# A planner that books a shared port from the third mixer on

## The chip, the cores and the metric

One core of one Trainium2 chip runs the kernel. The metric is the device time of one execution in microseconds; the time before is the median of three runs, 1043.78 us (1042.79 to 1044.37).

## The reference, cut to what matters

The reference is two transformer blocks on 256 tokens of width 1024. The first block has two layers: a mixer (FoX attention and sparse latent attention in the first, block attention in the second) and a feed-forward net with a short convolution. The second block has one layer, and the change begins with its mixer:

```python
c_q, c_kv, k_r, x_m, z, i_pre, f_pre = _split_in(h @ w_in[i])
attn_out = _mla_attention(q_nope, q_rope, k_nope, k_rope, v)      # 8 heads, run in 4 pairs
xc = jax.nn.silu(_causal_conv(x_m, conv_w[i], conv_b[i]))
hm = _mlstm_chunkwise(mq, mk, mv, ig, fg)                         # 4 heads
x = x + jnp.concatenate([attn_out, ml_out], axis=-1) @ w_o[i]
x = x + _hier_moe(...)                                            # 32 experts, 2 per token
x = x + (p[i] @ w_ple[i]) * jax.nn.sigmoid(hp @ w_ple_gate[i])
```

All is computed in float32; large products split each weight and each activation into a high and a low part and add three products (high by high, high by low, low by high).

## The kernel before, in words

The kernel is one straight program for 256 tokens. Activations lie with features on the partitions, weights stream from HBM through slots in SBUF (`Weights`, lines 209 to 346). For each unit of 1024 columns ScalarE casts the high part (`high`, line 291) and VectorE subtracts to get the low part (`low`, line 300). `W.eighths` says how many eighths of a low part go to GpSimd instead; it is 0 in the third mixer's dense products and 4 in the first half of its output projection (line 1159).

In a mixer the dense products (`product`, line 987) run on TensorE, and between them stand steps of side work. Each chain of side work is a Python generator: `mla` for a pair of attention heads (lines 1815 and 1085), `lstm_inputs` for the convolution and its Silu (line 1706), `mlstm` for an mLSTM head (line 1850), `lstm_outputs` and `gate_tiles` for its normalization and gate, `scale_x` for scaling the residual X (line 1662). `tick` (line 432) is called after every six matmuls of a dense product. It goes through the list of chains in order of priority and takes the next step of the first chains whose last result is foreseen to be ready by the foreseen time of TensorE (line 447), at most one step per tick here (`MOST`). `pause` (line 453) does the same with nothing else to issue, and moves the time on by 0.1 us if no chain is ready. So the order of instructions in every engine's queue is fixed when the program is built, by foreseen times.

The foreseen times come from `Clock` (line 64). `cost` (line 123) gives the duration of an operation by engine and columns, `issue` (line 148) starts it when its engine is free and its operands are ready, and `LATE` (line 67) is added before another engine may use the result. For n columns VectorE is given 0.07 + 0.00104 n us (0.0007 n for a copy or a scaling in SBUF) and GpSimd 0.1 + 0.0022 n; a matmul of 256 columns has 0.109. Engines do not disturb each other in `issue`.

The order of weight casts is decided apart: `prepare` (line 320) issues casts when the weights are there and a small number of units is ahead, and `take` (line 342) forces the unit that is to be used.

After the third mixer come the output projection with the router's inputs (`out_proj`, `to_moe`), the routing, a stage of 32 experts in a written order, and a last gated product. The numbers of most experts to load are known only after the routing (`order_of_use`, line 2142); until then only the first six experts' weights can be fetched.

Of the kernel before, what the change touches and what calls it, by code (L numbers as in the profile page):

```python
# [18 lines left out]
PSUM = bass.MemoryType.PSUM  # L19
# [44 lines left out]
class Clock:  # L64
# [6 lines left out]
    def __init__(self):  # L71
        self.at = dict.fromkeys(("pe", "act", "dve", "pool", "sp", "dma"), 0.0)
        self.log, self.rings, self.gone = {}, {}, set()
        self.last = self.floor = 0.0
        self.table, self.off = "-", False
        self.duty = {}

    def now(self):
        return max(self.at["pe"], self.floor)
# [43 lines left out]
    def cost(self, eng, what, outs, ins, func):  # L123
        n = max(self.size(x) for x in outs + ins)
        if eng == "pe":
            n = self.size(outs[0])
            if ins[0].dtype in (F32R, BF):
                return (max(n, 64) * 0.417e-3 + 0.0023) * (4 if n < 256 and ins[0].dtype == F32R else 1)
            if what == "transpose":
                return 0.109  # L130
            if self.box(outs[0])[0] >= 32:

                return 0.03
            return max(0.096, n * 1.667e-3 + 0.0023)
        if eng == "act":
            t = self.TABLES.get(func)
            c = (0.027 if ins[0].space == PSUM else 0.045) + n * 0.887e-3 + 0.1 * (len(ins) - 1) + 0.09 * (len(outs) - 1)
            if t and self.table not in t:
                self.table = t[0]
                c += 1.28  # L140
            return c
        if eng == "dve":
            mild = what in ("tensor_scalar", "tensor_copy") and all(x.space != PSUM for x in outs + ins)
            more = 0.06 if what != "tensor_tensor" and not mild and any(self.size(x) == 1 for x in ins) and n > 1 else 0
            return 0.07 + n * (0.7e-3 if mild else 1.04e-3) + more
        return 0.1 + n * 2.2e-3

    def issue(self, eng, what, outs, ins, func=None):
        for x in outs + ins:
            if x.tensor.name in self.gone:  # L150
                raise RuntimeError(f"{x.tensor.name} has been given up")
        if self.off:
            return
        s = max([self.at[eng]] + [self.ready(x, False, eng) for x in ins] + [self.ready(x, True, eng) for x in outs])
        if eng == "sp":
            self.at["sp"] = s + 0.45
            n = math.prod(c for _, c in outs[0].ap) * 4
            end = max(s + 1.2, self.at["dma"]) + n / 2 ** 20 * 2.91
            self.at["dma"] = end
            late = end + 0.5  # L160
        else:
            c = self.cost(eng, what, outs, ins, func)
            if eng == "pe":
                w = int(s / self.WINDOW)
                self.duty[w] = self.duty.get(w, 0.0) + c
                if self.duty.get(w - 1, 0.0) < self.BUSY * self.WINDOW:
                    c *= 2
            end = s + c
            late = end + self.LATE[eng]
            self.at[eng] = end  # L170
            self.last = max(self.last, late)
        for x in ins:
            self.note(x, False, end, late, eng)
        for x in outs:
            self.note(x, True, end, late, eng)
# [178 lines left out]
def tile_two_blocks(ctx: ExitStack, tc: tile.TileContext, a: dict, out: bass.AP):  # L354
    clk = Clock()
# [5 lines left out]
    def st(shape, dt=F32, tag=None, name=None, bufs=1):  # L361
        return sb.tile(list(shape), dt, tag=tag or name, name=name or tag, bufs=bufs)
# [238 lines left out]
    for i, g in enumerate(ORDER0):  # L601
        n = ORDER0[:i].count(g)
# [960 lines left out]
    for i, g in enumerate(ORDER0):  # L1563
        n = ORDER0[:i].count(g)
# [77 lines left out]


    lay[0] = W.phase = 2
    r4 = st([128, 4], name="r4")

    def norm_twice():
# [945 lines left out]
```

## Time and profile before

| | us |
|---|---|
| median of three runs | 1043.78 |
| profiled execution | 1051.57 |
| its span | 1049.9 |
| TensorE busy | 987.1 (94%) |
| VectorE busy | 620.6 (59%) |
| ScalarE busy | 479.7 (46%) |
| GpSimd busy | 98.1 (9%) |
| mean granted clock of TensorE | 0.968 of full speed |

PE is TensorE, PEld its weight loads, DVE is VectorE, ACT is ScalarE, POOL is GpSimd, SP issues the DMAs. Times in the views are in microseconds from the start of the span. Nearly all instructions have the line 205, that of a helper which records them, so they are told apart by the names of the tiles: `out<-in`. In the third mixer aP and aPT are softmax tiles, aQ and aR queries, keys and their rotations, bX and bZ the tiles of the mLSTM, `extra`, `wh`, `wl`, `xhw`, `xlw` high and low parts of weights, and `more` a wide tile with tables and masks.

### The profile page before, as it was taken

The numbers are of one execution on the slowest core, as the hardware profiler recorded it, in microseconds if no ns is written. First come the engines' busy times: TensorE is split into PE (matmuls) and PEld (weight loads), VectorE is DVE, ScalarE is ACT, GpSimd is POOL, SyncE is SP. The second block draws the span as 40 slices with busy tenths as digits, with TensorE's granted clock in tenths as the row PEclk, the third lists the DMA queues.
The fourth block names the chain that finished last, engine by engine and source line by source line (L and its number), as shares of the span: only waits on it lengthen the run. The fifth ranks groups of instructions, "written<-read, shape, count | busy, mean of one in ns | idle before, by whom it ended". The sixth has DMA issues, their size and how long they took to land.

```text
span 1049.9 us, 19301 instructions
## 1 busy us (share of the span) xinstructions
PE 987.1 (94%) x7612; PEld 851.0 (81%) x7612; DVE 620.6 (59%) x1285; ACT 479.7 (46%) x868; POOL 98.1 (9%) x183
## 2 busy tenths in 40 slices
PE   7999999999999999999999999979889999788697
PEld 7988899999999998999999999857775454343276
DVE  5698576666678588676666687685463122111046
ACT  5555565444555465564544465664422111111063
POOL 7414120000001000000000000040310000000001
PEclk8999999999999999999999999988889999998898
DMA  7563299564610632597556103423579899999961
GB/s 217 168 201 118 85 327 344 172 224 152 226 42 3 199 123 79 192 368 243 191 171 206 63 1 105 137 81 138 208 263 397 334 413 409 413 410 412 410 214 41
DMA packets 135313, 223.10 MB, mean 213 GB/s; under 512 B 11161, under 2 KB 103473, under 8 KB 135217
## 3 DMA queue, kind: packets, MB, share of 16 engines
q1 hardware_dynamic: 134673, 221.80, 59.3%
q8 instruction: 62, 1.02, 0.4%
q14 instruction: 34, 0.28, 0.1%
q10 hardware_dynamic: 544, 0.00, 0.0%
HBM read 220.73 MB, written 1.05 MB: 211 GB/s over the span
## 4 chain that ended last, share of the span: by engine, by line
PE 75%; DMA 12%; DVE 9%; ACT 3%; issue 1%; SPq 0%; POOL 0%; DVEq 0%; ACTq 0%
PE bank L205 75%; DMA w<-in_w_gate_e_dram 6%; DMA w<-in_w_down_e_dram 3%; DMA w<-in_w_up_e_dram 2%; DVE a L205 1%; DMA w<-in_w_in_even_dram 1%; DVE wl L205 1%; DVE X L205 1%; DVE mx L205 1%; DVE xl L205 1%; DVE extra L205 1%; DVE aR L205 1%; DVE gates L205 1%; DVE m L205 0%; ACT wh L205 0%
## 5 line engine op out<-in xcount | busy, mean ns | idle before, releaser
L205 PE MATMUL bank<-xh,wh 128*128 128x256 f32 x808 | 231.4, 286 | 3.1 <-ACT wh L205 3.1
L205 PE MATMUL bank<-xl,wh 128*128 128x256 f32 x808 | 226.4, 280 | 0.3 <-DVE xl L205 0.3
L205 PE MATMUL bank<-xh,wl 128*128 128x256 f32 (+1 forms) x752 | 211.2, 281 | 1.0 <-DVE wl L205 1.0
L205 ACT ACTIVATE wh<-w 128x1024 fp32r<-128x1024 f32 x153 | 159.8, 1051 | 6.2 <-PE bank L205 5.3
L205 PEld LDWEIGHTS bank<-xh,wh 128*128 128x128 f32 x808 | 153.6, 190 | 5.4 <-ACT wh L205 3.3
L205 PEld LDWEIGHTS bank<-xl,wh 128*128 128x128 f32 x808 | 153.4, 190 | 1.4 <-issue 0.7
L205 PEld LDWEIGHTS bank<-xh,wl 128*128 128x128 f32 (+1 forms) x752 | 142.4, 189 | 1.4 <-DVE wl L205 1.4
L205 PE MATMUL bank<-xh,extra 128*128 128x256 f32 (+1 forms) x552 | 141.9, 283 | 0.0
L205 DVE TENSOR_TENSOR wl<-w,wh 128x1024 fp32r<-128x1024 f32 (+2 forms) x102 | 120.1, 1178 | 8.0 <-ACT wh L205 6.5
L205 PE MATMUL bank<-w,xg 128*32 128x512 f32 (+1 forms) x512 | 93.4, 645 | 18.6 <-DMA w<-in_w_up_e_dram 12.4
L205 PEld LDWEIGHTS bank<-xh,extra 128*128 128x128 f32 (+1 forms) x552 | 98.6, 187 | 1.0 <-issue 0.9
L205 ACT ACTIVATE c<-more,v,cw 128x256 f32<-128x256 f32 x44 | 26.5, 603 | 137.6 <-DVE more L205 137.6
L205 PEld LDWEIGHTS bank<-w,xg 128*32 128x32 f32 (+1 forms) x512 | 30.3, 127 | 72.7 <-issue 71.5
L205 DVE TENSOR_TENSOR more<-bank,more 128x512 f32<-128x512 f32 x44 | 30.4, 692 | 80.5 <-PE bank L205 80.5
L205 PE MATMUL bank<-al,wh 128*128 128x256 f32 x256 | 71.5, 279 | 0.0
L205 PE MATMUL bank<-ah,wh 128*128 128x256 f32 x256 | 71.4, 279 | 0.0
L205 POOL TENSOR_TENSOR sq<-sq 128x512 f32<-128x512 f32 (+1 forms) x14 | 16.0, 1144 | 582.3 <-ACT sq L205 397.3
L205 PE MATMUL bank<-xl,extra 128*128 128x256 f32 (+2 forms) x248 | 69.8, 281 | 0.0
L205 DVE SCALAR_TENSOR_TENSOR sg<-sg,ws,bank 128x256 f32<-128x256 f32 x11 | 5.3, 481 | 107.1 <-ACT sg L205 107.1
L205 PE MATMUL bank<-ah,extra 128*128 128x256 f32 x256 | 65.6, 280 | 0.0
L205 DVE TENSOR_TENSOR extra<-w,wh 128x1024 fp32r<-128x1024 f32 (+2 forms) x51 | 60.8, 1192 | 3.3 <-ACT wh L205 3.3
L205 ACT ACTIVATE extra<-w 128x1024 fp32r<-128x1024 f32 (+4 forms) x54 | 53.5, 996 | 1.0 <-PE bank L205 0.9
(483 smaller groups left out, 2165.9 us busy)
## 6 DMA issues: line engine op xcount, KB each, us to landing
w<-in_w_up_dram SPq DMA_DIRECT2D x44, 1024.0 KB
w<-in_w_gate_e_dram SPq DMA_DIRECT2D x64, 512.0 KB
w<-in_w_up_e_dram SPq DMA_DIRECT2D x64, 512.0 KB
w<-in_w_down_e_dram SPq DMA_DIRECT2D x32, 1024.0 KB
w<-in_w_down_dram SPq DMA_DIRECT2D x22, 1024.0 KB
w<-in_w_in_odd_dram SPq DMA_DIRECT2D x12, 1024.0 KB
w<-in_w_in_even_dram SPq DMA_DIRECT2D x9, 1024.0 KB
w<-in_w_in_dram SPq DMA_DIRECT2D x5, 1024.0 KB
```

The lines of the kernel that those rows point to most:

```text
L205: return f(*a, **kw)
```

## The change

A flag `shared` is set where the third mixer begins, after line 1644, and stays set. With it, VectorE's cost per column rises from 0.00104 to 0.00113 us (copies and scalings in SBUF keep 0.0007). And `issue` keeps one time `port`: every GpSimd operation, and every VectorE operation with two or more operands in SBUF that are larger than one column, starts no sooner than `port` and moves it to its own end. The booking goes in the order in which the program issues the operations.

```diff
@@ class Clock, __init__
         self.duty = {}
+        self.shared, self.port = False, 0.0
@@ cost
-            return 0.07 + n * (0.7e-3 if mild else 1.04e-3) + more
+            return 0.07 + n * (0.7e-3 if mild else 1.13e-3 if self.shared else 1.04e-3) + more
@@ issue
                 if self.duty.get(w - 1, 0.0) < self.BUSY * self.WINDOW:
                     c *= 2
+            if self.shared and eng in ("dve", "pool"):
+
+                if eng == "pool" or sum(x.space != PSUM and self.size(x) > 1 for x in ins) > 1:
+                    s = max(s, self.port)
+                    self.port = s + c
             end = s + c
@@ after lay[0] = W.phase = 2
+    clk.shared = True
```

## Rows read from the trace of the kernel before

**Rows 1.** The page's chain that ended last, by engine.
```profile
PE 75%; DMA 12%; DVE 9%; ACT 3%; issue 1%; SPq 0%; POOL 0%; DVEq 0%; ACTq 0%
```

**Rows 2.** By stretch: length, busy PE, PEld, DVE, ACT, POOL, granted clock, DMA share, GB/s.
```profile
653.00:684.30 31.30, 31.14 (x230) 28.12 (x229) 21.26 (x48) 20.77 (x30) 4.25 (x5) 1.00 0.42 135
...
688.40:694.50 6.10, 0.01 (x1) 0.05 (x1) 6.07 (x10) 5.65 (x9) 3.78 (x3) 0.77 0.34 106
694.50:708.00 13.50, 13.42 (x70) 9.60 (x70) 11.16 (x22) 6.64 (x13) 5.02 (x4) 0.85 0.29 108
...
785.00:989.00 204.00, 182.61 (x1146) 91.12 (x1142) 36.89 (x117) 32.82 (x67) 0.00 (x0) 0.95 1.00 398
```

**Rows 3.** Timeline of the issuing queue around the routing: start, duration, instruction.
```profile
777.78 0.94 SPq L205 DMA_DIRECT2D w<-in_w_down_e_dram  x2
785.51 0.36 SPq L205 DMA_DIRECT2D w<-in_w_gate_e_dram  x1
```

**Rows 4.** Waits of PE from 655 to 745: us, times, longest.
```profile
PE bank L205 <- DVE aP L205: 6.1, 1, 6.1
```

**Rows 5.** Timeline of DVE from 660 to 713: start, duration, idle time before.
```profile
660.64 1.51 DVE L205 SCALAR_TENSOR_TENSOR bX<-bX,v 128x253 f32<-128x253 f32 x3
...
676.68 1.22 DVE L205 TENSOR_TENSOR extra<-w,wh 128x1024 fp32r<-128x1024 f32 x1
680.80 1.15 DVE L205 TENSOR_REDUCE mx<-bank 128x1 f32<-128x128 f32 x4 [2.90 <-PE bank L205]
681.98 1.21 DVE L205 TENSOR_SCALAR mx<-mx 128x4 f32<-128x4 f32 x1
683.10 2.62 DVE L205 SCALAR_TENSOR_TENSOR bX<-bX,v 128x253 f32<-128x253 f32 x3
685.64 1.22 DVE L205 TENSOR_TENSOR wl<-w,wh 128x1024 fp32r<-128x1024 f32 x1
...
693.85 0.16 DVE L205 RECIPROCAL ri<-sm 128x4 f32<-128x4 f32 x1
...
712.50 0.17 DVE L205 TENSOR_SCALAR mx<-mx 128x4 f32<-128x4 f32 x1
```

**Rows 6.** Timeline of POOL from 675 to 703.
```profile
675.86 0.60 POOL L205 COPY aQ<-aR 32x512 f32<-32x512 f32 x1
681.87 1.29 POOL L205 TENSOR_TENSOR bZ<-bZ 128x512 f32<-128x512 f32 x1 [5.41 <-issue]
...
700.80 1.60 POOL L205 TENSOR_TENSOR aQ<-aQ,aR 32x512 f32<-32x512 f32 x1 [3.80 <-DVE aR L205]
702.35 0.80 POOL L205 COPY aQ<-aR 32x512 f32<-32x512 f32 x1
```

**Rows 7.** Timeline of PE from 679 to 685.
```profile
679.17 1.47 PE L205 MATMUL bank<-aQ 96*128 96x256 f32 x8
...
680.88 0.28 PE L205 MATMUL bank<-xl,wh 128*128 128x256 f32 x1
...
684.17 0.28 PE L205 MATMUL bank<-xh,extra 128*128 128x256 f32 x1
```

**Rows 8.** Timeline of ACT from 678 to 685.
```profile
678.26 0.59 ACT L205 ACTIVATE bX<-bX,v 128x256 f32<-128x256 f32 x1
...
684.56 0.37 ACT L205 ACTIVATE aP<-bank,mx 128x128 f32<-128x128 f32 x1
```

**Rows 9.** Timelines of DVE and PE on the late chain, 723 to 750.
```profile
723.49 0.56 DVE L205 TENSOR_TENSOR bX<-bank,bX 128x384 f32<-128x384 f32 x1 [0.51 <-ACT bX L205]
...
726.66 1.08 PE L205 MATMUL bank<-aPT,w 128*64 128x256 f32 x4
731.13 0.83 PE L205 MATMUL bank<-V,bX 128*128 128x129 f32 x6
...
749.21 0.69 DVE L205 TENSOR_TENSOR ml<-mlo,mh 128x512 fp32r<-128x512 f32 x1 [0.70 <-ACT mh L205]
```

**Rows 10.** Timeline of DVE at the scalings of X.
```profile
701.29 4.73 DVE L205 SCALAR_TENSOR_TENSOR X<-X,v,more 128x256 f32<-128x256 f32 x6
```

## The prediction

> **What bounds the kernel now.** I read the chain of waits first: its engine line gives TensorE (PE) 75% and DMA 12% of the span [rows 1]. VectorE (DVE) has 9%, so a change that touches only what is foreseen of DVE and GpSimd (POOL) can pay only where those two are in the chain. The stretches from the third mixer on say where [rows 2]. From 653 to 684.3 us PE is busy 31.14 of 31.30 us: the dense products bound it, and no order of side work gains there. From 688.4 to 694.5 PE does nothing (0.01 of 6.10 us) while DVE is busy 6.07: DVE bounds. From 694.5 to 708 PE is busy again, at a granted clock of 0.85, so partly at the lower level. From 785 to 989 the DMA share is 1.00, at 398 GB/s: the expert weights bound, and their amount is fixed. The queue of the issuing engine shows that this stream cannot start sooner than the routing: after two weights at 777.78 the next goes out at 785.51 [rows 3], when the chosen numbers are known. So what the mixer gains or loses before 785 I pass on to the end one for one.
>
> The wait inside the mixer is one row: PE stood 6.1 us for aP, the softmax scaling of the first head pair [rows 4]. DVE's timeline says why [rows 5]. DVE stood idle 2.90 us until 680.80, then took the maxima, convolution steps and the low parts of weights for the output projection, and reached ri, the step ahead of aP, only at 693.85. In this stretch it is slower beside POOL: a scaling of 4 elements took 1.21 us at 681.98, against 0.17 at 712.50; three convolution steps took 2.62 at 683.10, against 1.51 at 660.64. POOL was at work on SBUF at 681.87 for 1.29 us [rows 6], and for 3.78 of the next stretch's 6.10 [rows 2].
>
> **The change, part by part.** It adds and removes no instruction and no DMA: every matmul, every DVE and POOL operation has the same shape and count. It changes what the planner books for an operation from line 1644 on, and so the place of side steps in the queues. Its cost is the cost of the places that move.
>
> (a) Column time. A low part of 1024 columns was booked at 0.07 + 1024 x 0.00104 = 1.135 us and is now 1.227; the trace has 1.22 [rows 5]. A matmul of 256 columns stays booked at 0.109, while 29 of them started from 680.88 to 684.17, so one each 0.1175 [rows 7]. Before, both were short by 7%; now only the matmul is, so DVE looks later against PE than it is, by some 8% of its backlog. In the dense stretch this moves steps by a tick (six matmuls, 0.7 us) here and there. PE is full, so I take 0; the ends are -0.2 (the stretch's idle time) and +1.4 (two ticks at its end).
>
> (b) The booked port. The first pair's scores need a POOL copy. That copy ran at 675.86 for 0.60 us [rows 6], beside the low part at 676.68 [rows 5]. Now it is booked behind the low part: 677.90 + (0.1 + 512 x 0.0022 = 1.23) + 0.20 = 679.33. The scores were issued at 679.17 [rows 7], so they miss that tick and go one or two later; I take two, 1.4 us. In those two ticks the next in the list are the first three convolution steps, whose input ScalarE (ACT) gives from 678.26 for 0.59 us [rows 8]. So DVE fills its idle time: the steps from 678.9 to 680.4 (1.51, nothing of POOL beside them), the low part of 685.64 to about 681.6, the maxima from 682.2 to 683.4, their scaling to 683.5 (0.17) or 684.6 (1.21). Before, these four were done at 686.86, so DVE is 2.2 to 3.3 us ahead. ACT's exp starts 0.3 to 1.3 us later than its 684.56 [rows 8], which holds back the casts that the last halves wait for; going down the queue I get ri at about 691.7 against 693.85. **I take -2.2 us; the ends are 0 and -3.3.**
>
> By the Trainium skill (SBUF — State Buffer, "Who interferes with whom") a tensor_scalar can hold the pair of ports too, which the change does not book; the 1.21 us for 4 elements agrees with it, and the sum by it is the end at 2.2, by the booked port the one at 3.3.
>
> (c) The rest of the stall stays. The four low parts that stand ahead of ri are taken in one go when the output projection begins: lines 1160 and 325 to 335 look at the arrival of weights, not at DVE or POOL. A planner that foresees the full wait (its booked sum for this stretch rises from about 7.8 to about 13 us, and the trace has 13.05 from 680.80 to 693.85) still has no PE work to put there: the next products wait for a Silu behind the same queue. So 0 beyond (b); a gain past 3.3 is excluded by that.
>
> (d) The chains from 694.5 to 749.3. Here POOL has few operations and the new column time adds under 0.1 us a step, a fraction of a tick. I take 0. The ends are the rivals' prices, -4.4 and +4.7. What follows, the output projection's second half and the final stage, has written orders or few choices: 0, within 0.5.
>
> The sum is -2.2 us. The profiled execution took 1051.57 us (a span of 1049.9 and 1.67 around it), 7.79 over the median of 1043.78; taken as a shift, it becomes 1049.4 there and 1041.6 in the median. About 0.2%, or 2.1 us, is what a measurement of this kernel can tell from no change, so the forecast lies on that edge.
>
> **Rivals.**
> *Nothing decisive moves.* The moved scores land in the same idle time, the exp's delay eats what DVE gained, and the stall stays at 6.1: 1043.8, within 1 us. For it: (c), and the casts of ACT that the halves wait for. Against it: the 2.90 us idle and the missed tick.
>
> *The late chain is re-ordered for the better.* The product of x of the third mLSTM head is on DVE at 723.49 for 0.56 us, but PE uses it only at 731.13, 7.1 us later, and the fourth head follows behind it; from there runs the chain to the last ml at 749.21 [rows 9]. If PE takes that product at 726.7, where it now takes keys of the last pair, the tail comes 4.4 us sooner; with (b) this gives 1043.78 - 2.2 - 4.4 = 1037.2. For it: the wait is one of list order and not of data. Against it: nothing in this stretch contends, and priorities stay.
>
> *Slower: the port is booked where it is free.* The second and third pairs need POOL's additions, booked at 1.23 a piece and in the order in which the program issues them. The eight scalings of X each read two tensors in SBUF and now hold the port; six of them took 4.73 us from 701.29 [rows 10]. If they are issued ahead of POOL's additions, the planner holds the pairs' scores back for up to the 4.73 us, although POOL's own copy at 702.35 took only 0.80 [rows 6], and PE has little else. It decides once the scores of the second pair fall behind the last scaling by more than one tick. Price +4.7, less 2.2 where (b) holds: 1046.3; alone 1048.5. Against it: PE was busy 13.42 of 13.50 us there [rows 2], so it has other work for part of the wait.
> The Trainium skill (the same page and section) says that issue order decides who blocks, which speaks for this rival: program order is not the order of starts. The trace agrees that POOL's addition at 700.80 stretched to 1.60.
>
> **How the numbers follow.** Forecast 0.36 (-1 to -4 us, centre 1041.6; somewhat over half of it below the edge of 2.1), nothing moves 0.18, better late chain 0.18, slower 0.28. Faster by over 0.2%: 0.22 + 0.18 = 0.40; same: 0.14 + 0.18 = 0.32; slower 0.28. The range goes from the better chain's time to the lone slower one's, cut by half a microsecond each: 1036.7 to 1048.0, which leaves out some 2 in 10. Since both signs hold much, the forecast's own range is 1040 to 1043.
>
> **What would show it.** In the profile after: the convolution steps on DVE ahead of the first maxima; DVE's idle time before them under 1.5 us; ri one to three us sooner against the end of the dense products, and PE's wait for aP 3 to 5 us; the third head's product within a tick or two of where it is; DMA's full stretch equally long and sooner by the gain. Wrong: the wait at 6 us or more, the six scalings of X ahead of POOL's additions with PE idle after them, or a shift that begins after 785.

## The result, and the profile after

The changed kernel takes 1042.99 us (median of 20 runs, 1041.34 to 1047.86). The kernel before, run beside it, has a median of 1050.45 (20 runs, 1042.73 to 1052.66), and the ratio over the executions is 0.9949 with a 95% interval of 0.9933 to 0.9965: faster by half a per cent (the means differ by 5.1 us, the medians by 7.46). The time lies 1.4 us above the forecast of 1041.6 and inside its range. One thing must be known to read the ratio: runs of the kernel before fall in two groups, near 1044 and near 1051, and the three shown ahead of the prediction were all of the lower group; the profiled execution (1051.57) is of the upper one.

The profiled execution after took 1043.06 us, 8.51 less than that of before. The chain that ended last, by engine, answers to [rows 1]:

```profile
PE 70%; DMA 12%; DVE 11%; ACT 3%; issue 2%; POOL 1%; SPq 0%; DVEq 0%; ACTq 0%; POOLq 0%
```

The windows of after answer to [rows 2]; the columns are the same. The first row reaches from the dense products of the third mixer (640 us; PE is busy without a gap from there to 653 us in every execution told of here) to the first step of the norm ahead of the router.

```profile
640.00:767.13 127.13, 114.97 (x816) 100.58 (x816) 86.32 (x211) 64.90 (x134) 30.25 (x50) 0.96 0.46 160
653.00:679.00 26.00, 23.90 (x182) 21.77 (x180) 15.80 (x34) 16.63 (x26) 1.64 (x2) 1.00 0.38 122
684.99:691.04 6.05, 5.23 (x32) 4.44 (x30) 5.98 (x8) 5.92 (x11) 4.28 (x3) 1.00 0.00 0
691.04:708.00 16.96, 14.89 (x77) 11.11 (x78) 11.42 (x34) 9.55 (x29) 4.89 (x5) 0.90 0.36 124
776.92:979.92 203.00, 181.79 (x1144) 90.59 (x1140) 36.63 (x115) 32.82 (x67) 0.00 (x0) 0.95 1.01 400
```

The same two stretches of the kernel before, and the one from the end of its dense products to 708 us:

```profile
640.00:774.19 134.19, 118.61 (x809) 103.84 (x809) 86.66 (x209) 69.47 (x137) 29.70 (x50) 0.92 0.43 151
653.00:679.00 26.00, 25.84 (x186) 22.94 (x185) 17.83 (x41) 17.03 (x27) 1.82 (x2) 1.00 0.38 122
684.30:708.00 23.70, 17.48 (x92) 12.67 (x90) 21.22 (x36) 16.38 (x33) 10.03 (x8) 0.86 0.26 89
```

From this follow three readings. The weights' stream is as long as before (203.0 us at a DMA share of 1.01) and only starts sooner. From 640 us to the router's norm after needs 7.06 us less. Of these, 3.42 are idle time of PE (134.19 - 118.61 = 15.58 before, 127.13 - 114.97 = 12.16 after), and 3.64 are busy time, for the same matmuls at a granted clock of 0.96 instead of 0.92. And the dense stretch from 653 to 679 got worse: PE is busy 23.90 us of 26 where it had 25.84.

The issuing queue passes the gain on: the weight that waits for the routing goes out at 777.13 instead of 785.51 [rows 3], 8.38 us sooner, nearly the whole of the 8.51.

```profile
777.13 0.36 SPq L211 DMA_DIRECT2D w<-in_w_gate_e_dram  x1
```

PE's waits from 650 to 745 us (in total, times, longest) answer to [rows 4]; the one of 6.1 us is gone, and no single one is above 1.6:

```profile
PE bank L211 <- ACT bX L211: 3.5, 5, 1.4
PE bank L211 <- DVE aQ L211: 1.6, 1, 1.6
```

DVE's timeline after answers to [rows 5, 9, 10]; `ml` is the low part of the mixer's output, which the rest of the output projection needs:

```profile
679.20 1.51 DVE L211 SCALAR_TENSOR_TENSOR bX<-bX,v 128x253 f32<-128x253 f32 x3
...
686.44 2.74 DVE L211 TENSOR_SCALAR bZ<-bX,v 128x256 f32<-128x256 f32 x2
...
701.57 1.15 DVE L211 TENSOR_REDUCE mx<-bank 128x1 f32<-128x128 f32 x4 [3.55 <-PE bank L211]
...
707.12 0.14 DVE L211 RECIPROCAL ri<-sm 128x4 f32<-128x4 f32 x1
...
715.70 2.00 DVE L211 SCALAR_TENSOR_TENSOR X<-X,v,more 128x256 f32<-128x256 f32 x2
...
743.99 0.42 DVE L211 TENSOR_TENSOR ml<-bank,mh 128x256 fp32r<-128x256 f32 x1 [1.92 <-ACT mh L211]
```

The convolution steps stand ahead of the first maxima, as forecast, but the maxima come 21 us later than before (701.57 against 680.80) and ri 13 us later. The first attention pair was not moved by a tick or two; it went behind the stall. PE's timeline says what stands in its place. `more,mk` are the scores of an mLSTM head, `aQ` those of an attention pair:

```profile
688.27 1.95 PE L211 MATMUL bank<-w,bX 128*128 128x128 f32 x16
691.04 0.92 PE L211 MATMUL bank<-more,mk 128*128 128x256 f32 x4 [0.82 <-ACT mk L211]
...
699.85 1.57 PE L211 MATMUL bank<-aQ 96*128 96x256 f32 x8
...
721.90 0.92 PE L211 MATMUL bank<-more,mk 128*128 128x256 f32 x4
723.93 1.55 PE L211 MATMUL bank<-aQ 96*128 96x256 f32 x8
```

In the kernel before, the first mLSTM head and the last of both lots stood here:

```profile
705.45 0.92 PE L205 MATMUL bank<-more,mk 128*128 128x256 f32 x4
...
729.18 1.47 PE L205 MATMUL bank<-aQ 96*128 96x256 f32 x8
732.15 0.82 PE L205 MATMUL bank<-more,mk 128*128 128x256 f32 x4
```

So the two lots of side work changed places: the mLSTM's products, which need only the convolution and its Silu, fill the time in which the low parts of the output projection hold DVE, and the last of the eight heads' and pairs' scores starts at 723.93 instead of 732.15.

### The profile page after: what moved, and what is told of

Read it like the earlier page. It is cut to its first block, busy times and chain, and to the rows that moved or that the text cites. A ratio compares the mean times of both kernels' runs of the same rounds, so it can differ in the third digit from the quotient of the medians.

```text
span 1041.3 us, 19299 instructions
## 1 busy us (share of the span) xinstructions
PE 982.3 (94%) x7612; PEld 846.0 (81%) x7612; DVE 620.9 (60%) x1285; ACT 475.1 (46%) x865; POOL 98.4 (9%) x183
## 4 chain that ended last, share of the span: by engine, by line
PE 70%; DMA 12%; DVE 11%; ACT 3%; issue 2%; POOL 1%; SPq 0%; DVEq 0%; ACTq 0%; POOLq 0%
PE bank L211 70%; DMA w<-in_w_gate_e_dram 6%; DMA w<-in_w_down_e_dram 3%; DMA w<-in_w_up_e_dram 2%; DVE wl L211 1%; DVE aR L211 1%; DVE X L211 1%; DVE a L211 1%; DVE extra L211 1%; DMA w<-in_w_in_even_dram 1%; DVE bX L211 1%; DVE xl L211 1%; DVE gates L211 1%; DVE mx L211 1%; ACT wh L211 0%
## 5 line engine op out<-in xcount | busy, mean ns | idle before, releaser
L211 PE MATMUL bank<-w,xg 128*32 128x512 f32 (+1 forms) x512 | 95.5, 657 | 20.0 <-DMA w<-in_w_up_e_dram 19.9
```

What stands on the lines that cost most here:

```text
L211: return f(*a, **kw)
```

## Experiments

The theory after the result: the gain is one of order. The mLSTM's products go into the stall, PE idles less, and the granted clock stays higher; whether the booked durations are true does not matter. The rivals: a truer foresight pays by itself; the gain is the contention of DVE and POOL that the new order avoids; it is the granted clock alone. e1 to e4, e5 to e8 and e9 to e11 were each run beside the kernel before, which had medians of 1050.42, 1051.09 and 1049.34 us; each ratio is to the runs beside it.

**e1_cols** keeps the new column time and takes the port's booking out.

```diff
-            if self.shared and eng in ("dve", "pool"):
+            if False and eng in ("dve", "pool"):
```

> The changed kernel with the port taken out: only the column time of 0.00113 us is kept. Theory A (the gain comes from where the first head pair's attention stands: behind the half low parts of the output projection's weights, so that TensorE no longer stands 6.1 us for its softmax scaling): in this order the first scores come after the dense products too, so the wait for aP is under 1.5 us and the time is 3 to 7 us under the kernel before. Theory B (the booked port makes the gain): within 2 us of the kernel before. Theory C (any other order gives another time, by chance): somewhere within 8 us of it on either side, with no link to the wait.

Measured: 1045.57 us (1043.56 to 1046.66), ratio 0.9954 (0.9927 to 0.9982). The column time alone moves the first pair's scores from 679.17 to 697.88 and the first mLSTM head's to 691.7. So the theory that the booked port makes the gain (theory B) falls, and theory A has its time. But PE still has a long wait, of 4.4 us, only later (at 735.77, for aPT). The column time also costs time in the dense stretch:

```profile
640.00:770.15 130.15, 116.66 (x818) 102.42 (x819) 84.89 (x210) 65.29 (x134) 31.12 (x50) 0.94 0.45 160
653.00:679.00 26.00, 23.89 (x182) 21.86 (x182) 15.78 (x37) 16.71 (x25) 1.29 (x1) 1.00 0.38 122
```

The loss from 653 to 679, 1.95 us of PE's time against the kernel before, is the same as after (1.94).

**e2_port** keeps the booking and takes the column time out.

```diff
-            return 0.07 + n * (0.7e-3 if mild else 1.13e-3 if self.shared else 1.04e-3) + more
+            return 0.07 + n * (0.7e-3 if mild else 1.04e-3) + more
```

> The changed kernel with the old column time: only the port is kept. The prediction's step (b) says: the first scores one or two ticks later, DVE 2.2 to 3.3 us ahead, the wait for aP 3 to 5 us, the time 2.2 us under the kernel before. Theory A: the first scores stay ahead of the dense products' end, so the wait for aP stays at 4 to 6 us and the time is within 3 us of the kernel before. Theory B: all of the gain, 5 us or more.

Measured: 1041.51 us (1038.26 to 1043.10), ratio 0.9905 (0.9878 to 0.9932). This run holds what the prediction's step (b) told, by itself. DVE and PE:

```profile
679.93 1.52 DVE L211 SCALAR_TENSOR_TENSOR bX<-bX,v 128x253 f32<-128x253 f32 x3 [0.98 <-ACT bX L211]
682.55 1.15 DVE L211 TENSOR_REDUCE mx<-bank 128x1 f32<-128x128 f32 x4 [1.10 <-PE bank L211]
...
692.83 1.75 DVE L211 TENSOR_TENSOR extra<-w,wh 128x512 fp32r<-128x512 f32 x1
...
695.03 0.16 DVE L211 RECIPROCAL ri<-sm 128x4 f32<-128x4 f32 x1
```

```profile
680.93 1.25 PE L211 MATMUL bank<-aQ 96*128 96x256 f32 x6
...
693.59 3.47 PE L211 MATMUL bank<-bX,w 128*128 128x256 f32 x8 [4.19 <-ACT bX L211]
```

The scores come 1.76 us later (680.93 against 679.17), the convolution steps fill the idle time, and the maxima follow. But ri is not sooner, and PE does not wait for it: it takes the mLSTM's products of the Silu's result (`bX,w`) as soon as the Silu is there, after 4.19 us, and the softmax products behind them. PE loses nothing in the dense stretch:

```profile
640.00:765.89 125.89, 113.74 (x818) 101.27 (x818) 88.16 (x210) 69.29 (x137) 30.84 (x50) 0.97 0.46 163
653.00:679.00 26.00, 25.84 (x186) 22.96 (x185) 18.88 (x43) 16.93 (x26) 1.83 (x2) 1.00 0.39 122
```

**e3_hold** undoes the whole change and instead has the attention pairs wait, by a written condition, for the last dense product.

```diff
-        launch(mla(i), ("t4", "kv", "q"))
+        launch(mla(i), ("t4", "kv", "q", "dense"))
...
+    state.add("dense")
```

> The kernel before with its old costs; the attention pairs are launched only after the last dense product has been issued. Theory A: no wait for aP over 1.5 us and 4 to 8 us under the kernel before, with no better foresight at all. Theory B: no gain, since the port is not booked. Theory C: anything within 8 us.

Measured: 1039.03 us (1038.35 to 1042.07), ratio 0.9896 (0.9870 to 0.9922). With the old foreseen times, and the mLSTM first, it beats both kernels, by more than theory A's 4 to 8 us (11.4 in the medians).

```profile
640.00:764.19 124.19, 113.77 (x819) 101.15 (x818) 83.24 (x211) 66.67 (x135) 31.59 (x50) 0.97 0.47 165
653.00:679.00 26.00, 26.00 (x204) 24.43 (x203) 18.95 (x43) 21.29 (x32) 2.24 (x3) 1.00 0.42 132
```

PE is busy through the whole dense stretch (26.00 of 26), and idles 10.42 us in all up to the norm.

**e4_early** does the opposite: the changed kernel, with the first pair and the chain of its queries put ahead by priority (parts of the long line `PRI`).

```diff
-'mla0': -1, 'ckv2_chain': -1}
+'mla0': -3, 'ckv2_chain': -1, 'cq_chain': -3}
```

> The changed kernel with its new costs; the priorities of the query chain and of the first attention pair are raised, so that the pair's scores come ahead of the end of the dense products again, as before the change. Theory A: TensorE again waits 4 to 7 us for aP and the time is 3 to 7 us over the changed kernel. Theory B: within 2 us of the changed kernel.

Measured: 1055.15 us (1052.28 to 1057.13), ratio 1.0044 (1.0026 to 1.0063). It is 12.2 us slower than the changed kernel, more than theory A's 3 to 7, and not by a return of the wait for aP (1.3 us at the longest). PE's longest waits from 650 to 755 us:

```profile
PE bank L211 <- ACT aQ L211: 5.5, 1, 5.5
PE bank L211 <- ACT mh L211: 4.4, 2, 2.2
PE bank L211 <- ACT bX L211: 3.7, 5, 1.8
```

The first mLSTM head comes at 720.64 (705.45 in the kernel before) and the last at 737.79 (732.15). The longest wait has another name than in the kernel before; the heads are late in both.

**e5_mfirst** gives the kernel before another order by priorities alone: the mLSTM's inputs first (a part of the line `PRI`).

```diff
-{'mlstm1': 1, 'lstm_outputs0': -2, 'lstm_inputs1': -1,
+{'mlstm1': 1, 'lstm_outputs0': -2, 'lstm_inputs0': -3, 'lstm_inputs1': -3,
```

> The kernel before with its old costs; only the priorities of the two mLSTM input chains are raised (to -3). Theory A2 (after the first runs: the gain comes from the mLSTM heads' scores being sooner, at 691 to 703 us instead of 705 and 718, so that their chains run beside the attention pairs; the wait for aP is only one sign of it): first two heads scored before 700 us, the router's norm starts at 764 to 768 instead of 774, the time 6 to 12 us under the kernel before. Theory B (better foresight of the port and of DVE is what pays): within 2 us of the kernel before. Theory C (chance): anything within 10 us.

Measured: 1043.33 us (1041.78 to 1046.09), ratio 0.9949 (0.9926 to 0.9971): the ratio of the change, without its foresight. The first two heads come at 694.80 and 696.59. Theory B falls by this run: the old costs, in another order, give as much. Theory A2 has the heads and the time, but not the norm, which starts at 769.83 and not at 764 to 768.

**e6_wrong** makes the foresight worse: no port, and a column time of 0.00095, below the measured one.

```diff
-            return 0.07 + n * (0.7e-3 if mild else 1.04e-3) + more
+            return 0.07 + n * (0.7e-3 if mild else 0.95e-3 if self.shared else 1.04e-3) + more
...
+    clk.shared = True
```

> The kernel before with VectorE's column time made worse instead of better from the third mixer on: 0.00095 us a column (booked 1.04 for 1024 columns, measured 1.22), and no port. Theory B (foresight pays): slower than the kernel before by 2 us or more. Theory A2: the planner puts the first heads' scores later than before, so they come after 710 us, and the time is 2 to 8 us over the kernel before. Theory C (any re-ordering, gains as likely as losses): as likely faster.

Measured: 1057.85 us (1052.84 to 1060.27), ratio 1.0081 (1.0052 to 1.0111). The first head comes at 716.05, the last at 740.34. A wrong cost of this sign hurts, as the theory of foresight has it too; the run alone does not tell the two apart, since it also puts the heads late.

**e7_nopool** takes POOL's half of the low parts away in the first half of the output projection of the kernel before, so that DVE does them alone.

```diff
-            W.eighths = 4
+            W.eighths = 0
```

> The kernel before with all low parts of the output projection's first half on VectorE, none on GpSimd. It takes away most of the GpSimd work beside which VectorE was slow, and gives VectorE four halves more (4 x 0.60 = 2.4 us by rows). If the contention itself costs the time: DVE reaches ri no later than before and the time is the same or 1 to 3 us less. If not: ri 1 to 2 us later and the time 1 to 3 us more. Order changes little in either case.

Measured: 1047.35 us (1042.12 to 1050.74), ratio 0.9981 (0.9953 to 1.0008), an interval that holds 1. POOL's busy time from 640 us to the norm falls from 29.70 to 19.55 us, and PE's idle time from 15.58 to 15.14. ri came no later, though DVE had the four halves more:

```profile
693.13 0.17 DVE L205 RECIPROCAL ri<-sm 128x4 f32<-128x4 f32 x1
```

By the expectation this is the side on which the contention costs DVE time: leaving it out pays for the four halves. But PE still waits 5.7 us for aP, and the time is not told from before's. This edit takes contention away and gives DVE work at once, so it does not price the contention by itself. e2 says more against the rival: there three low parts ran at 1.75 to 1.77 us beside POOL, where the kernel before has one, and it is faster. The contention that an order avoids is not what makes the gain.

**e8_again** is the kernel before with nothing changed, once, for the two groups of its executions.

> The kernel before once more, with a profile. Its runs fall into two groups, near 1043 and near 1051 us. If this one falls near 1043: theory D1 (the TensorE clock) says that the stretch from the last ml to the routing is 2 to 3 us shorter at a granted clock nearer 1.0; theory D2 says the wait for aP is shorter; either shows at which stage the groups part. If it falls near 1051, it repeats the profile of before within 1 us at every stage.

Measured: 1044.41 us, one of the lower group, 7.16 below the profile shown ahead of the prediction, with the same order of instructions. PE's stall is the same in it and in the other execution, 6.15 us and 6.14:

```profile
693.88 1.51 PE L205 MATMUL bank<-ident,aP 128*128 128x128 f32 x6 [6.15 <-DVE aP L205]
```

```profile
694.49 1.51 PE L205 MATMUL bank<-ident,aP 128*128 128x128 f32 x6 [6.14 <-DVE aP L205]
```

Four windows of it, and the last three of the other execution:

```profile
640.00:769.62 129.62, 112.97 (x806) 98.99 (x804) 86.27 (x206) 69.31 (x137) 30.23 (x50) 0.96 0.44 155
694.00:698.00 4.00, 4.00 (x19) 2.65 (x19) 3.89 (x12) 1.58 (x3) 1.27 (x1) 0.63 0.93 347
704.00:712.00 8.00, 6.18 (x38) 4.64 (x37) 4.16 (x13) 5.17 (x15) 0.00 (x0) 1.00 0.01 2
712.00:720.00 8.00, 8.00 (x55) 6.52 (x54) 6.21 (x22) 4.87 (x19) 0.03 (x1) 1.00 0.00 0
```

```profile
694.00:698.00 4.00, 3.52 (x12) 2.36 (x13) 3.86 (x14) 1.06 (x3) 1.27 (x1) 0.50 1.03 373
704.00:712.00 8.00, 6.93 (x33) 5.18 (x32) 3.26 (x8) 4.36 (x8) 0.55 (x1) 0.79 0.00 0
712.00:720.00 8.00, 8.00 (x44) 6.63 (x44) 4.95 (x20) 4.69 (x20) 0.00 (x0) 0.78 0.01 2
```

PE's idle time is the same within 1.1 us (16.65 and 15.58), but after the stall one execution runs at a granted clock of 1.00 and the other at 0.79 and 0.78, and PE's busy time differs by 5.64 us (112.97 and 118.61). So theory D2 falls, and D1 holds but tells only a part: from the last ml to the weight that waits for the routing e8 takes 33.58 us (745.92 to 779.50) and the other 35.61 (749.90 to 785.51), at granted clocks of 0.97 and 0.86: 2.03 of the 7.16 us. Of the rest, 0.61 is there before the stall ends, 3.37 come between the stall and the last ml, at the clocks above, and 1.15 behind the routing. The two groups differ in the clock after the stall; what decides which one an execution gets is not settled.

Against an execution of the lower group the change gains 1.35 us (1043.06 and 1044.41), not 8.51: up to the norm 4.49 us less idle time of PE, and 2.00 more busy time at the same mean clock; behind the norm 1.14 are lost again. The median of before is of the upper group, so the ratio of 0.9949 holds the clock's share too: 14 of the 20 executions of before took over 1047 us, and of the 20 after only one (1047.86). By these counts the larger part of the gain is that the lower clock comes less often; that the change saves time at an equal clock is not shown, since 1.4 us is less than the executions of one kernel differ by. For the hold of e3 it is: its six executions took at most 1042.07 us, and the fastest of all the executions of the kernel before 1042.34.

**e9_holdport, e10_holdafter and e11_hold_again** put the port's booking, and the whole change, on top of the hold of e3, and repeat e3 beside them.

Their edit of the kernels of e2 (for e9), after (for e10) and before (for e11) is that of e3:

```diff
-        launch(mla(i), ("t4", "kv", "q"))
+        launch(mla(i), ("t4", "kv", "q", "dense"))
...
+    state.add("dense")
```

> The first pair is held until the last dense product, as in e3, and the port is booked as in e2 (column time as before). In the plan all four heads of the mLSTM now come ahead of the first pair's scores, where e3 has two pairs between the second and the third head. Theory A (what counts is how soon the last of the four mLSTM heads starts; its scores came at 719.4 in e3, 719.6 in e2, 721.9 after, 729 to 732 before): the last head's scores come before 712, the last ml at or before e3's 740.1, and the time is 1036 to 1039. Theory B (both lots of side work must be interleaved, whichever comes last sets the end): the pairs now come last, the last ml lands at 744 to 748 and the time is 1042 to 1046. Theory C (foreseeing the port is what pays, and adds to the hold): below 1037, with PE waiting under 3 us in one piece.

> The first pair is held until the last dense product on top of the whole change (port and column time). The change has the first pair's scores at 699.85, later than the hold would ask, so the hold changes little but the pair's preparation. Theory A (last mLSTM head): as e9, 1036 to 1040. Theory B (interleaving): the plan has the four heads first and the pairs last, so 1042 to 1046. Theory C (foresight adds to the hold): below 1039.0, the time of e3, and no slower than e9.

> The kernel of e3 once more, so that e9 and e10 are compared with it on the same chip: 1039.0 within 1.5, a ratio to the kernel before of 0.987 to 0.993. If e3's time was luck of the chip or of the granted clock, 1042 or more.

Measured: e9 1038.86 us (1037.30 to 1041.66), ratio 0.9907 (0.9876 to 0.9938); e10 1048.24 (1044.99 to 1050.99), ratio 0.9994 (0.9972 to 1.0017); e11 1039.34 (1037.58 to 1041.25), ratio 0.9907 (0.9876 to 0.9937). The hold repeats. Theory C falls: on top of the hold the booked port gives nothing (1038.86 and 1039.34), and the measured column time costs 9.4 us. Theory A gave e9's time, but not for its reason: e9's last mLSTM head starts at 706.18, 12.6 us sooner than e11's 718.77, and the time is the same; and in e10, with that head at 708.91, it expected 1036 to 1040 and is wrong by 8 us. Theory B named the side of e10, with 1042 to 1046 too low, and missed e9, where pairs come last but not late. Nor did the plan come out as expected: in both, the trace has two pairs (698.44 in e9, 700.09 in e10) ahead of the fourth head. PE in e9:

```profile
706.18 0.82 PE L211 MATMUL bank<-more,mk 128*128 128x256 f32 x4
...
725.98 1.54 PE L211 MATMUL bank<-aQ 96*128 96x256 f32 x8 [0.24 <-ACT aQ L211]
```

and in e10, where it waits 4.81 us in one piece for DVE's output steps, after which the last two pairs come late:

```profile
708.91 0.81 PE L211 MATMUL bank<-more,mk 128*128 128x256 f32 x4
...
722.19 1.55 PE L211 MATMUL bank<-aPT,V 128*64 128x256 f32 x8 [4.81 <-DVE ml L211]
...
734.76 1.47 PE L211 MATMUL bank<-aQ 96*128 96x256 f32 x8
```

What fits the thirteen profiled executions best is the idea behind theory B: the end goes with the last of the eight starts, whichever lot it is of. No edit moves that start alone, so this is a reading of the table and not shown as a cause, and e2 is an exception: its start is later than that of four slower executions. "Last start" is the later of the last pair's and the last head's scores; idle and busy are PE's from 640 us to the norm; all in us.

| kernel | profiled time | last start | last ml ends | PE idle | PE busy | granted clock |
|---|---|---|---|---|---|---|
| e9 hold + port | 1038.25 | 725.98 | 741.37 | 11.09 | 111.52 | 0.99 |
| e3 hold | 1038.96 | 722.14 | 740.14 | 10.42 | 113.77 | 0.97 |
| e11 hold again | 1041.25 | 721.52 | 739.52 | 11.22 | 113.92 | 0.97 |
| e2 port alone | 1041.44 | 730.55 | 747.06 | 12.15 | 113.74 | 0.97 |
| after | 1043.06 | 723.93 | 744.41 | 12.16 | 114.97 | 0.96 |
| e8 before, lower | 1044.41 | 728.96 | 745.92 | 16.65 | 112.97 | 0.96 |
| e5 mLSTM first | 1044.93 | 729.34 | 745.14 | 12.10 | 117.73 | 0.95 |
| e1 columns alone | 1046.23 | 727.19 | 750.64 | 13.49 | 116.66 | 0.94 |
| e10 hold + change | 1047.69 | 734.76 | 750.21 | 16.45 | 114.48 | 0.95 |
| e7 no POOL | 1047.97 | 730.99 | 749.23 | 15.14 | 117.60 | 0.94 |
| before, upper | 1051.57 | 732.15 | 749.90 | 15.58 | 118.61 | 0.92 |
| e4 pair first | 1055.51 | 737.79 | 754.74 | 20.48 | 119.18 | 0.90 |
| e6 wrong columns | 1058.12 | 740.34 | 760.39 | 19.96 | 123.72 | 0.86 |

The last ml ends 15.4 to 20.5 us after the last start in all but e1 (23.5). PE's idle time and the clock, which mostly goes with it (not in e8 and e10), make up the time (idle and busy time are the whole stretch up to the norm): from the norm to the end all thirteen take 274.4 to 277.4 us.

## Why the prediction was right, and where it was wrong

**The time and the sign** came out: 1042.99 in a range of 1036.7 to 1048.0, and faster. In this there is luck, since the gain came by another way than the forecast one, a shorter wait for aP. The size depends on what it is set against. The forecast was a gain of 2.2 us from 1043.78, a time of the lower group, and from there it is 0.8. From before's median over 20 runs it is 7.46 us, and 0.5% by the ratio. Taking the profiled execution's 7.79 us over the median as a shift that stays was the mistake of reading: e8, the same kernel, takes 7.16 us less, and most of the difference comes behind the stall, at a higher clock; and after runs at 0.96 up to the norm and not at 0.92.

**(a) Column time, put at 0 with an upper end of +1.4: mis-sized twice.** In the dense stretch it costs 1.95 us of PE's time (e1) and 1.94 (after), above its end. And it does not move steps "by a tick here and there": alone it takes the first pair 18.7 us back (679.17 to 697.88), and the time comes down by 0.46%. `tick` is written so that a chain that misses its tick is overtaken by others. That the 18.7 us came about in this way is argued from the code; no run here follows the plan tick by tick.

**(b) The booked port, -2.2: the mechanism was right, the way of its gain was not.** In e2 the scores miss two ticks (1.76 us, forecast 1.4), the convolution steps go where DVE idled, its idle time in one piece falls from 2.90 us [rows 5] to 1.10, and PE's longest wait to 4.19, inside the forecast 3 to 5. But ri came at 695.03, not 691.7: three low parts beside POOL's half took 1.75 to 1.77 us each where only one had in the kernel before. PE's wait is shorter because another product ends it. Set against the lower group (e8's 1044.41) e2 gains 2.9 us, near the 2.2, so the size came out for another reason than the one given. In the kernel with both parts, the column time sets the place of the pair and step (b) is hardly seen: the maxima are at 701.57.

**(c) The rest of the stall, put at 0: this step failed.** The prediction said that a planner "still has no PE work to put there: the next products wait for a Silu behind the same queue". It held the order of the chains fixed. Once, in the changed kernel, the pair's exp and casts are not ahead of the Silu in ACT's queue, and its maxima not ahead of the convolution on DVE, the mLSTM's products are there. The Silu (`bX<-bX` on ACT) starts at 683.99 after, and stood at 692.66 before:

```profile
683.99 0.63 ACT L211 ACTIVATE bX<-bX 128x512 f32<-128x512 f32 x1 [2.70 <-DVE bX L211]
```

```profile
692.66 0.63 ACT L205 ACTIVATE bX<-bX 128x512 f32<-128x512 f32 x1
```

PE is busy 20.12 us of the 23.01 from 684.99 to 708 (5.23 and 14.89), against 17.48 of 23.70 before. No wait of 3 to 5 us for aP is left there, none at all is above 1.6, and the idle time of the stall fell by 3.33 us (6.22 to 2.89). The 7.46 us between the medians lie past the excluded 3.3, with the clock's share in them; against the lower group the gain stays inside.

**(d) The late chains, put at 0** with ends of -4.4 and +4.7: the last start came 8.2 us sooner (5.0 against e8). The rival of the better late chain had the place right (the third mLSTM head's product, 731.13 before [rows 9], now at 717.03) and the wrong cause: not a tick's choice there, but that the first head began 14 us sooner (691.04 against 705.45), and the others with it.

**The slower rival** did not come in the changed kernel: the eight scalings of X were put behind the first pair's maxima, between 712 and 724 us, two at a time, and no PE wait of over 1.6 us follows. That a price such as its own was possible is seen in e10 (1048.24), by another wait.

**What the change says of itself.** True durations were not what paid, though they are what the change is about. The port alone is worth 8.9 us in the medians (1050.42 to 1041.51), the columns alone 4.9, both together 7.5, less than the port alone (all three hold the clock's share, and against e8's 1044.41 they are 2.9, -1.2 and 1.4); with the pairs held the port is worth nothing and the columns cost 9.4. Effects that do not add, and that change sign with what is fixed beside them, are what a re-ordering gives. One condition that holds the pairs back gives more than the change, with the old costs: 1039.03 and 1039.34.

That POOL holds DVE up in the way the change books is true all the same: a half low part took 1.75 us beside POOL's half in e2, and 0.68 alone (at 692.39, after). There is also a case that the change does not book, since one of the two operands is a single column: after, two scalings of 256 columns took 2.74 us at 686.44, beside two low parts on POOL, and in e2, with POOL between two operations, the same two took 0.60:

```profile
686.44 1.30 POOL L211 TENSOR_TENSOR xhw<-w,xhw 128x512 fp32r<-128x512 f32 x1 [2.82 <-ACT xhw L211]
687.70 1.34 POOL L211 TENSOR_TENSOR xlw<-w,xlw 128x512 fp32r<-128x512 f32 x1
```

By the Trainium skill (SBUF — State Buffer, "Who interferes with whom") such a scaling can take the shared pair of ports and then waits out the other's whole instruction; the 2.74 us against POOL's 2.60 agree with it.

## What to carry to other kernels

Where a planner picks the next step by foreseen times, a cost is a tie-breaker: compute which chain overtakes which, not how many tenths a step is booked longer, and look at the last chain to start and at PE's idle time when an order is to be priced. Profile two executions before a difference of some us is put down to an order: here the same program differed by 7.16. When the profile names one wait, ask which other chain could run in it before calling it fixed. If a change of costs pays, look for the order that it happened on and write that order down: here one condition was worth more than the truer costs, and adding the costs to it lost the gain.

## What was not expected of the hardware

The same program ran its third mixer at two granted clocks: after a stall of 6.1 us in which PE did next to nothing, both executions show 0.50 and 0.63 (the level of 1.2 GHz, fully or in part) from 694 to 698 us, and then one has 1.00 (2.4 GHz) from 704 to 720 while the other has 0.79 and 0.78. PE's busy time up to the norm differs by 5.64 us for it, the whole time by 7.16, about as much as the two medians of the result. In the six profiled executions with the least idle time of PE up to the norm (10.42 to 12.16 us) the mean clock from 640 us to the norm was 0.95 to 0.99, and their kernels' medians are below 1044; e8, with 16.65 us idle and 0.96, shows that more idle time does not always bring a lower clock.
